# PSUM places for the second MLP matrix: a pair's three sums in three single banks, two-bank places kept for the inner tiles and the last transposes

## The chip, the cores and the metric

The kernel runs on one core of a Trainium2 chip. TensorE (PE in the profile) multiplies matrices and writes only to PSUM, the accumulation memory; VectorE (DVE) and ScalarE (ACT) read PSUM and do everything elementwise; GpSimd (POOL) does small elementwise work and issues some DMAs; SyncE (SP) issues the rest. Engines run on their own and wait for each other by semaphores. PSUM is used here in eight banks, each holding 512 floats for every one of 128 partitions. The metric is the time of one execution in device microseconds (us); less is better.

## The reference

One step of a decoder layer for 512 prompt tokens and 8 sample tokens (520 columns), width 1024, in float32. The change lies in the last part, the MLP and the final normalisation:

```python
h2 = _rmsnorm(x, norm2_g[l]) * (1.0 + sc2) + sh2
ff = jnp.square(jax.nn.relu(h2 @ w_ff1[l])) @ w_ff2[l]     # w_ff1 1024 x 4096, w_ff2 4096 x 1024
x = x + g2 * ff
y = _rmsnorm(x, final_norm_g)
```

The parts before it (a combined input projection, two recurrences, their merge and the output projection) are untouched.

## The kernel before

**Products.** Activations are kept transposed: features on partitions, the 520 tokens as columns, in two halves of 260 (`HALF`). Every float32 product is made of three faster ones, with the weight and the activation each split in a high and a low part: high by high, high by low, low by high (`products` L110, and the loop in `product` L1087). A weight tile comes by DMA into `wst`; ScalarE copies its high part (`whi`, L75), VectorE subtracts for the low part (`wlo`, L78). Smaller ones are `xhi` and `xlo` (L1033, L1036).

**The MLP in quarters.** The 4096 inner features are cut in four quarters `q` of eight tiles `j`. `unit(q, j, c)` (L1063) is a quarter of one inner tile: 12 matmuls into a two-bank place, one bank per half of the tokens; four of them make the tile. `hidden` (L1116) and `squared` (L1162) then evacuate it: a small ScalarE copy (`fsh`, L1159), a VectorE multiplication by the norm's factor (`ft`, L1172), ReLU and square on ScalarE. `formed` turns two tiles into seven combinations of them, for the next step.

**The second matrix, by seven products.** For each quarter, the output's eight 128-row tiles are taken in four pairs `m`. A pair by two halves of the tokens is a 2 by 2 block product, computed by Strassen's scheme (Winograd's form) with seven products instead of eight. Each product (`product`, L1074) is 12 matmuls of 128x128 by 128x260: four inner steps of three. The seven, numbered 1 to 7 in the code, go into three sums:

- sum 0: products 1, 6, 5, 3, one after the other onto the same accumulator,
- sum 1: products 7, then 4,
- sum A: product 2 alone.

Between two products of one sum, the intermediate value is read out: ScalarE copies it to SBUF (`snap`, L1098; L1106 scales, L1108 does the eight sample columns), after products 1, 6, 7 and 5. After 2 and 4 VectorE adds it to `x` at once (L1214), after 3 also (L1226, L1227). GpSimd adds the snaps to `x` by DMAs that accumulate (L1202, L1220).

**The order** is written out in `plan` (L916) and kept by `behind`, so TensorE runs the items in that order. In quarters 0 to 2, after the inner tiles, the products of pair `m` are woven with the last two of pair `m - 1`:

```python
prods(q, (0, 6), (0, 2), (0, 7), (0, 5))
for m in range(1, 4):
    prods(q, (m, 1), (m - 1, 4), (m - 1, 3), (m, 6), (m, 2), (m, 7), (m, 5))
units(q + 1, 1, 0)
prods(q, (3, 4), (3, 3))
```

Three units of the next quarter stand within this stretch, two after product (0, 1) and one before (3, 4). In the last quarter the order is another, since its last inner tile is needed soon after it is done: (0, 1) and (1, 1), then the first three inner steps of (0, 2), (1, 2), (0, 7), (1, 7), then their last steps, then the rest. `schedule` (L969) gives the item at which each weight is split; the order on ScalarE, VectorE and for other transposes follows from the compiler's own list schedule by priority, in which `urgent` (L149) moves instructions ahead.

**PSUM in the MLP.** The tile framework gives out places of pools and adds the waits. `ppt` and `ppb` have one bank each, `pmm` two places of two banks, and `pps`, two single banks, is closed at the start of the MLP so that `pm3`, a third two-bank place, can lie there (L1246). `place` (L1057) hands out the three two-bank places in turn: to the inner tiles, and to a pair for sums 0 and 1, one in each bank (`t[:, 0], t[:, 1]`, L1081). Sum A goes to `ppt` or `ppb` in turn.

**The end.** When a pair of output tiles is complete, `final_pair(m, s)` (L1302) transposes its 256 rows back to tokens for half `s` of the tokens, four transposes into bank `s` of one place per pair (`fplace`); ScalarE sums squares (L1318), VectorE multiplies by the final gain (`fx`, L1326). With `s` = 1 the samples follow in a bank of `ppt` (L1322 to L1325). `final_rows` (L1329) scales the rows and sends them out.

Of the kernel before, what the change touches and what calls it, by code (L numbers as in the profile page):

```python
# [6 lines left out]
F32 = mybir.dt.float32  # L7
# [4 lines left out]
OP = mybir.AluOpType  # L12
PSUM = bass.MemoryType.PSUM
# [3 lines left out]
L = 512  # L17
NB = 8
T = L + NB
HALF = T // 2  # L20
# [28 lines left out]
class Kernel:  # L49
# [19 lines left out]
    def _split_w(self, st, place, after=None):  # L69
        if place is None:  # L70
            hi, lo = (self.wst.tile([128, KO, 128], F32R, tag="wst", name=n) for n in ("whi", "wlo"))
        else:
            pool = self.sw if place % 2 else self.whl
            hi, lo = (pool.tile([128, KO, 128], F32R, tag=f"{n}{place}", name=n, bufs=1) for n in ("whi", "wlo"))
        ins = self.nc.scalar.copy(hi, st)  # L75
        if after:
            self.behind(ins, after)
        self.nc.vector.tensor_tensor(lo, st, hi.bitcast(F32), OP.subtract)  # L78
        return hi, lo
# [974 lines left out]
    def entry(self, key):  # L1054
        return self.ready[key[1:]]

    def place(self, n=None):  # L1057

        if n is None:
            n = self.nplace = (self.nplace + 1) % 3  # L1060
        return (self.pmm if n else self.pm3).tile([128, 2, 512], F32, name="mm")

    def unit(self, q, j, c):  # L1063

        if c == 0:
            self.upsum = self.place()
        hi, lo = self.entry(self.tile_key(q, j))
        for k in (2 * c, 2 * c + 1):
            last = self.last_product
            self.products(self.upsum, (hi[:, k], lo[:, k]), self.h2[k], k == 0, k == KO - 1, NM + 1, after=last)  # L1070
        if c == 3:
            self.hidden(q, j, self.upsum)

    def product(self, q, m, j, ks):  # L1074

        st = self.pairs.setdefault((q, m), {"s": {}})
        g, part = self.GROUP[j]
        hi, lo = self.entry(self.pair_key(q, m, g))
        if ks[0] == 0:
            if j == 1:  # L1080
                t = self.place((self.nplace + 2) % 3 if (q, m) == (3, 3) else None)  # L1081
                st["mm"] = t[:, 0], t[:, 1]
            if j == 2:
                st["A"] = (self.ppt.tile([128, 512], F32, name="pt") if m % 2 and (q, m) != (3, 3) else
                           self.ppb.tile([128, 512], F32, name="pb"))
        ps = (st["A"] if j == 2 else st["mm"][int(j in (7, 4))])[:, :HALF]
        for k in ks:  # L1087
            w, (ah, al) = 4 * part + k if g else k, self.ff[k]
            f = self.FORM[j]
            for n, (x, y) in enumerate(((hi, ah), (hi, al), (lo, ah))):  # L1090
                ins = self.nc.tensor.matmul(ps, x[:, w], y[:, f], start=j in (1, 7, 2) and k == 0 and n == 0,  # L1091
                                            stop=k == 3 and n == 2, skip_group_check=True)
                self.behind(ins, self.last_product)
                self.last_product = ins
        if ks[-1] == 3:
            self.added(q, m, j, ps, st["s"])
# [65 lines left out]
    def squared(self, q, j, ps, sh, halves):  # L1162
        nc = self.nc
        a, n = halves[0], len(halves)
        c = slice(a * HALF, (a + n) * HALF)
        if a == 0:
            self.ft = self.misc.tile([128, T], F32, name="ft", bufs=2)
        t, u = self.two(self.ft)[:, a:a + n], ps[:, a:a + n, :HALF]
        if q == 0 and j < 2:
            nc.scalar.copy(t, u)  # L1170
            u = t
        nc.vector.tensor_tensor(t, u, self.two(self.rs)[:, a:a + n], OP.mult)  # L1172
        t = self.ft[:, c]
        p = min(c.stop, L) - c.start
        nc.scalar.activation(t[:, :p], t[:, :p], AF.Relu, bias=sh[:, 0:1])  # L1175
        if c.stop == T:
            eng = nc.vector if j == KO - 1 else nc.gpsimd
            eng.tensor_tensor(t[:, p:], t[:, p:], sh[:, 1:9], OP.add)  # L1178
            eng.tensor_scalar(t[:, p:], t[:, p:], 0.0, None, OP.max)
        f = self.f8[:, 2 * (j % 2) + a:2 * (j % 2) + a + n]  # L1180
        nc.scalar.activation(f, self.two(self.ft)[:, a:a + n], AF.Square)  # L1181
# [54 lines left out]
    def mlp(self):  # L1236
        nc, tc = self.nc, self.tc
        self.close_pool()
        self.early.close()
        self.ffp = self.ctx.enter_context(tc.tile_pool(name="ffp", bufs=1, reuse_waits="tile"))  # L1240
        self.zs = self.consts.tile([128, KO, NB], F32, name="zs")
        nc.vector.memset(self.zs, 0.0)
        self.ng = self.consts.tile([128, KO], F32, name="ng")
        nc.vector.tensor_scalar(self.ng, self.modT[:, 40:48, 0], -1.0, None, OP.mult)
        self.ff, self.pairs = {}, {}
        self.pp.close()  # L1246
        self.pm3 = self.ctx.enter_context(tc.tile_pool(name="pm3", bufs=1, space=PSUM, reuse_waits="tile"))
        self.nplace, self.through, self.last_copy = 0, set(), None
        self.begin_weights()
        for n, (what, q, a, b, *ks) in enumerate(self.items):  # L1250
            self.ahead(n)
            if what == "u":
                self.unit(q, a, b)
                continue
            if what == "f":
                if q < 4:
                    self.ff[0] = self.ff_tiles(0)
                    self.formed(0, 0)
                    self.formed(0, 1)
                continue  # L1260
            if (q, a, b, ks[0][0]) == (3, 0, 1, 0):
                self.final_open()
            self.product(q, a, b, *ks)
# [38 lines left out]
    def final_pair(self, m, s):  # L1302


        nc = self.nc
        self.njunk = (self.njunk + 1) % 4
        junk = self.junk[:, self.njunk]
        if s == 0:
            self.fplace = self.place((self.nplace + (0 if m == 3 else 1)) % 3)
        p = self.fplace[:, s]  # L1310
        p4 = p.rearrange("p (t m f) -> p t m f", t=2, m=2)
        fs = slice(2 * m * 128, 2 * m * 128 + 256)
        for j in range(2):
            for t in range(2):
                c = (2 * s + t) * 128
                nc.tensor.transpose(p4[:, t, j], self.x[2 * m + j][:, c:c + 128], self.ident)
        for t in range(2):
            nc.scalar.activation(junk, p[:, 256 * t:256 * t + 256], AF.Square,  # L1318
                                 accum_out=self.fss[:, 2 * s + t, m:m + 1])
        if s:  # L1320
            p2 = self.ppt.tile([128, 512], F32, name="pt")
            for j in range(2):  # L1322
                nc.tensor.transpose(p2[:NB, j * 128:(j + 1) * 128], self.x[2 * m + j][:, L:], self.ident)
            nc.scalar.activation(junk[:NB], p2[:NB, :256], AF.Square, accum_out=self.fss[:NB, NC, m:m + 1])
            nc.vector.tensor_tensor(self.fxs[:, fs], p2[:NB, :256], self.gbc[:NB, fs], OP.mult)  # L1325
        nc.vector.tensor_tensor(self.fx[:, 2 * s:2 * s + 2, fs], p.rearrange("p (t f) -> p t f", f=256),  # L1326
                                self.gbc[:, None, fs].to_broadcast([128, 2, 256]), OP.mult)
# [19 lines left out]
    def run(self):  # L1347
        tc, i, enter = self.tc, self.i, self.ctx.enter_context
# [5 lines left out]
        self.ppt = enter(tc.tile_pool(name="ppt", bufs=1, space=PSUM))  # L1354
        self.ppb = enter(tc.tile_pool(name="ppb", bufs=1, space=PSUM))
        self.pmm = enter(tc.tile_pool(name="pmm", bufs=2, space=PSUM))
        self.pp = ExitStack()
        self.pps = self.pp.enter_context(tc.tile_pool(name="pps", bufs=2, space=PSUM))
        self.whl = enter(tc.tile_pool(name="whl", bufs=2))
        self.act = enter(tc.tile_pool(name="act", bufs=2))  # L1360
        self.early = ExitStack()
# [187 lines left out]
```

## Time and profile before

| | us |
|---|---|
| median of 3 runs | 1072.58 (1072.53 to 1072.72) |
| the profiled execution, its own time | 1072.83 |
| its span in the profile | 1070.8 |
| granted TensorE clock, mean | 0.996 |
| busy: PE, DVE, ACT, POOL | 1012.6, 696.0, 526.0, 112.0 |
| inner tiles of quarters 1 and 2, stretches of the span | 778.78 to 821.46, 874.73 to 917.43 |
| products of quarters 0, 1 and 2 | 725.49 to 778.78, 821.46 to 874.73, 917.43 to 970.72 |
| products of the last quarter | 1010.46 to 1058.75 |
| after the last product | 1058.75 to 1070.8 |

How to read it: the span counts from the first instruction of the program, and the execution's own time has about 2 us around it. "Busy" of PE is the union of its matmuls' durations, which overlap: a matmul of 260 columns is shown with 0.28 us, and in a steady stream one starts every 0.12 us. So a short idle time of PE in the rows stands for a somewhat longer loss of its rhythm. In the lists of waits, a row gives the waiting instruction, who released it, the sum of the idle time, the times it occurred and the longest.

### The profile page before, as it was taken

The numbers are of one execution on the slowest core, as the hardware profiler recorded it, in microseconds if no ns is written. First come the engines' busy times: TensorE is split into PE (matmuls) and PEld (weight loads), VectorE is DVE, ScalarE is ACT, GpSimd is POOL, SyncE is SP. The second block draws the span as 40 slices with busy tenths as digits, with TensorE's granted clock in tenths as the row PEclk, the third lists the DMA queues.
The fourth block names the chain that finished last, engine by engine and source line by source line (L and its number), as shares of the span: only waits on it lengthen the run. The fifth ranks groups of instructions, "written<-read, shape, count | busy, mean of one in ns | idle before, by whom it ended". The sixth has DMA issues, their size and how long they took to land.

```text
span 1070.8 us, 24259 instructions
## 1 busy us (share of the span) xinstructions
PE 1012.6 (95%) x9940; PEld 970.0 (91%) x9940; DVE 696.0 (65%) x1583; ACT 526.0 (49%) x1020; POOL 112.0 (10%) x215
## 2 busy tenths in 40 slices
PE   3899999999999999999999999999899889989995
PEld 1799999999999999999999999998899889989985
DVE  6568679596786867473333357766567656757765
ACT  5445744663574464351222244565456446545644
POOL 2200000000000000110000000022311321232030
PEclk9999999999999999999999999999999999999998
DMA  9963344344334335785555594224642562462142
GB/s 276 250 172 105 117 133 121 118 127 125 107 120 129 92 105 149 211 264 154 158 160 160 162 283 121 80 79 89 138 129 60 123 162 71 95 142 61 60 79 80
DMA packets 247792, 143.71 MB, mean 134 GB/s; under 512 B 6622, under 2 KB 242326, under 8 KB 247674
## 3 DMA queue, kind: packets, MB, share of 16 engines
q1 hardware_dynamic: 237874, 130.28, 42.7%
q0 software_dynamic: 9808, 11.89, 6.0%
q8 instruction: 78, 1.28, 0.5%
q14 instruction: 32, 0.26, 0.1%
HBM read 123.61 MB, written 11.26 MB: 126 GB/s over the span
## 4 chain that ended last, share of the span: by engine, by line
PE 87%; issue 3%; DMA 3%; ACT 3%; SPq 3%; DVE 2%; DVEq 0%; POOL 0%; ACTq 0%; POOLq 0%
PE mm L115 64%; PE mm L1091 11%; PE ps L356 2%; SPq L1441 2%; PE pb L702 1%; PE ps L561 1%; PE pb L1091 1%; ACT whi L75 1%; PE pt L1091 1%; DMA wst<-in_w_in_dram 1%; DMA wm<-in_w_mod_dram 1%; PE pt L645 1%; PE pt L634 1%; DVE ma L1214 1%; DMA wst<-in_w_out_dram 1%
## 5 line engine op out<-in xcount | busy, mean ns | idle before, releaser
L115 PE MATMUL mm<-h,whi 128*128 128x260 f32 (+1 forms) x3072 | 514.0, 286 | 1.4 <-ACT X L137 1.4
L115 PEld LDWEIGHTS mm<-h,whi 128*128 128x128 f32 x3072 | 427.3, 188 | 7.0 <-issue 3.4
L115 PE MATMUL mm<-h,wlo 128*128 128x260 f32 (+1 forms) x1536 | 316.4, 285 | 0.0
L75 ACT CAST whi<-wst 128x1024 fp32r<-128x1024 f32 x168 | 175.5, 1048 | 239.9 <-PE mm L115 173.9
L78 DVE TENSOR_TENSOR wlo<-wst,whi 128x1024 fp32r<-128x1024 f32 x168 | 205.1, 1221 | 115.8 <-ACT whi L75 114.6
L115 PEld LDWEIGHTS mm<-h,wlo 128*128 128x128 f32 x1536 | 239.9, 189 | 1.6 <-issue 1.0
L115 PE MATMUL mm<-a,whi 128*128 128x260 f32 x512 | 84.7, 285 | 0.0
L115 PEld LDWEIGHTS mm<-a,whi 128*128 128x128 f32 x512 | 70.6, 188 | 1.4 <-issue 1.4
L115 PE MATMUL mm<-a,wlo 128*128 128x260 f32 x256 | 52.3, 284 | 0.0
L1091 PE MATMUL mm<-ff0h,whi 128*128 128x260 f32 x80 | 26.0, 324 | 21.5 <-DVE ma L1214 13.6
L797 POOL DMA_DIRECT2D t<-oaT_d x8 | 4.3, 548 | 399.2 <-ACT ma L137 388.6
L1186 DVE TENSOR_TENSOR f<-f 128x260 f32<-128x260 f32 x64 | 27.3, 426 | 27.7 <-ACT f L1181 27.1
L115 PE MATMUL mm<-b,whi 128*128 128x260 f32 x256 | 41.8, 285 | 0.0
L1178 POOL TENSOR_TENSOR ft<-ft,fsh 128x8 f32<-128x8 f32 x28 | 17.5, 624 | 225.9 <-DVE ft L1172 225.9
L1175 ACT ACTIVATE ft<-ft,fsh 128x512 f32<-128x512 f32 (+2 forms) x36 | 23.9, 675 | 34.6 <-DVE ft L1172 34.6
L1091 PEld LDWEIGHTS mm<-ff0h,whi 128*128 128x128 f32 x80 | 15.0, 187 | 27.4 <-DVE ma L1214 16.5
L115 PEld LDWEIGHTS mm<-a,wlo 128*128 128x128 f32 x256 | 39.5, 188 | 0.2 <-issue 0.2
L115 PEld LDWEIGHTS mm<-b,whi 128*128 128x128 f32 x256 | 35.0, 188 | 1.6 <-issue 1.6
L1106 ACT ACTIVATE snap<-mm,ng 128x260 f32<-128x260 f32 (+1 forms) x30 | 14.3, 476 | 37.8 <-PE mm L1091 37.8
L1220 POOL DMA_DIRECT2D ma<-snap x28 | 25.6, 913 | 56.8 <-issue 41.0
L813 DVE TENSOR_TENSOR t<-mm,t 128x520 f32<-128x520 f32 x8 | 5.6, 699 | 36.7 <-PE ps L372 36.7
L1202 POOL DMA_DIRECT2D ma<-snap x28 | 25.0, 893 | 41.4 <-ACT snap L1108 17.9
(431 smaller groups left out, 1877.6 us busy)
## 6 DMA issues: line engine op xcount, KB each, us to landing
wst<-in_w_in_dram SPq DMA_DIRECT2D x64, 512.0 KB
wst<-in_w_mod_dram SPq DMA_DIRECT2D x32, 512.0 KB
wst<-in_w_ff_dram SPq DMA_DIRECT2D x64, 256.0 KB
wst<-in_w_ff_dram SPq DMA_DIRECT2D x32, 512.0 KB
wm<-in_w_mod_dram SPq DMA_DIRECT2D x16, 512.0 KB
st<-in_state_hgrn_dram SPq DMA_DIRECT2D x8, 512.0 KB
vb<-vd SPq DMA_DIRECT2D x8, 512.0 KB
out_dram<-st SPq DMA_DIRECT2D x8, 512.0 KB
```

Source lines behind the costliest of these rows:

```text
L75: ins = self.nc.scalar.copy(hi, st)
L78: self.nc.vector.tensor_tensor(lo, st, hi.bitcast(F32), OP.subtract)
L115: self.last_product = self.nc.tensor.matmul(ps[:, s, :c.stop - c.start], x, y[:, c], start=first and n == 0, stop=last and n == 2)
L356: nc.tensor.matmul(ps[r:r + 32, :n], self.cT[:, k, :], w[:, k, :], start=k < 4, stop=k >= KO - 4)
L1091: ins = self.nc.tensor.matmul(ps, x[:, w], y[:, f], start=j in (1, 7, 2) and k == 0 and n == 0, stop=k == 3 and n == 2, skip_group_check=True)
L1106: ins = self.nc.scalar.activation(t[:, :n], ps[:, :n], AF.Copy, scale=scale)
L1175: nc.scalar.activation(t[:, :p], t[:, :p], AF.Relu, bias=sh[:, 0:1])
L1178: eng.tensor_tensor(t[:, p:], t[:, p:], sh[:, 1:9], OP.add)
L1186: self.nc.vector.tensor_tensor(f[:, n], f[:, a], f[:, b], op)
L1202: nc.gpsimd.dma_start(x[1][:, b], v[:, :n], accum_op=OP.add)
L1220: nc.gpsimd.dma_start(x[t][:, a], s[p], accum_op=OP.add)
L1441: nc.sync.dma_start(raw[k][:, :, j * 128:(j + 1) * 128], w[r:r + 1024, c:c + 128].rearrange("(k p) n -> p k n", p=128))
```

## The change

PSUM in the MLP is laid out anew. `pps` stays open, and `pm3` and `place` go. Inner tiles take the two places of `pmm` in turn. A pair's three sums lie in three tiles of one bank each: sum 0 in `pps` (two banks, so two pairs may be open), sum 1 in `ppt`, sum A in `ppb`. Three sums of the last quarter, whose order keeps more of them open, take a whole `pmm` place and use its first bank. In the final step each `final_pair` takes a `pmm` place of its own, with the samples' transposes in its second bank, issued before the sums of squares instead of after. The multiplication that evacuates an inner tile is marked urgent for all tiles (before, for the last tile of a quarter alone).

```diff
     def unit(self, q, j, c):
         if c == 0:
-            self.upsum = self.place()
+            self.upsum = self.pmm.tile([128, 2, 512], F32, name="mm")
...
     def product(self, q, m, j, ks):
-        if ks[0] == 0:
-            if j == 1:
-                t = self.place((self.nplace + 2) % 3 if (q, m) == (3, 3) else None)
-                st["mm"] = t[:, 0], t[:, 1]
-            if j == 2:
-                st["A"] = (self.ppt.tile([128, 512], F32, name="pt") if m % 2 and (q, m) != (3, 3) else
-                           self.ppb.tile([128, 512], F32, name="pb"))
-        ps = (st["A"] if j == 2 else st["mm"][int(j in (7, 4))])[:, :HALF]
+        bank = {7: 4, 6: 1, 5: 1, 3: 1}.get(j, j)
+        if ks[0] == 0 and j in (1, 7, 2):
+            if (q, m, j) in ((3, 1, 7), (3, 1, 2), (3, 2, 1)):
+                st[bank] = self.pmm.tile([128, 2, 512], F32, name="mm")[:, 0]
+            else:
+                pool, name = {1: (self.pps, "ps"), 4: (self.ppt, "pt"), 2: (self.ppb, "pb")}[bank]
+                st[bank] = pool.tile([128, 512], F32, name=name)
+        ps = st[bank][:, :HALF]
...
     def squared(self, q, j, ps, sh, halves):
-        nc.vector.tensor_tensor(t, u, self.two(self.rs)[:, a:a + n], OP.mult)
+        with self.urgent():
+            nc.vector.tensor_tensor(t, u, self.two(self.rs)[:, a:a + n], OP.mult)
...
     def mlp(self):
-        self.pp.close()
-        self.pm3 = self.ctx.enter_context(tc.tile_pool(name="pm3", bufs=1, space=PSUM, reuse_waits="tile"))
...
     def final_pair(self, m, s):
-        if s == 0:
-            self.fplace = self.place((self.nplace + (0 if m == 3 else 1)) % 3)
-        p = self.fplace[:, s]
+        t = self.pmm.tile([128, 2, 512], F32, name="mm")
+        p, p2 = t[:, 0], t[:, 1]
...
+        if s:
+            for j in range(2):
+                nc.tensor.transpose(p2[:NB, j * 128:(j + 1) * 128], self.x[2 * m + j][:, L:], self.ident)
         for t in range(2):
             nc.scalar.activation(junk, p[:, 256 * t:256 * t + 256], AF.Square,
                                  accum_out=self.fss[:, 2 * s + t, m:m + 1])
         if s:
-            p2 = self.ppt.tile([128, 512], F32, name="pt")
-            for j in range(2):
-                nc.tensor.transpose(p2[:NB, j * 128:(j + 1) * 128], self.x[2 * m + j][:, L:], self.ident)
             nc.scalar.activation(junk[:NB], p2[:NB, :256], AF.Square, accum_out=self.fss[:NB, NC, m:m + 1])
```

More of the change, by code (lines that the diff above doesn't have):

```diff
@@ L1055, in entry @@
         return self.ready[key[1:]]
[L1057 to L1061, printed above, removed]
     def unit(self, q, j, c):
         if c == 0:
-            self.upsum = self.place()
+            self.upsum = self.pmm.tile([128, 2, 512], F32, name="mm")
         hi, lo = self.entry(self.tile_key(q, j))
@@ L1245, in mlp @@
         self.ff, self.pairs = {}, {}
-        self.pp.close()
-        self.pm3 = self.ctx.enter_context(tc.tile_pool(name="pm3", bufs=1, space=PSUM, reuse_waits="tile"))
-        self.nplace, self.through, self.last_copy = 0, set(), None
+        self.through, self.last_copy = set(), None
         self.begin_weights()
@@ L1356, in run @@
         self.pmm = enter(tc.tile_pool(name="pmm", bufs=2, space=PSUM))
-        self.pp = ExitStack()
-        self.pps = self.pp.enter_context(tc.tile_pool(name="pps", bufs=2, space=PSUM))
+        self.pps = enter(tc.tile_pool(name="pps", bufs=2, space=PSUM))
         self.whl = enter(tc.tile_pool(name="whl", bufs=2))
```

## The prediction

> **What bounds the kernel now.** I read the page first: who is busy, what the chain that ended last consists of, and the costliest groups.
>
> ```profile
> span 1070.8 us, 24259 instructions
> ...
> PE 1012.6 (95%) x9940; PEld 970.0 (91%) x9940; DVE 696.0 (65%) x1583; ACT 526.0 (49%) x1020; POOL 112.0 (10%) x215
> ...
> PE 87%; issue 3%; DMA 3%; ACT 3%; SPq 3%; DVE 2%; DVEq 0%; POOL 0%; ACTq 0%; POOLq 0%
> ...
> L1091 PE MATMUL mm<-ff0h,whi 128*128 128x260 f32 x80 | 26.0, 324 | 21.5 <-DVE ma L1214 13.6
> ```
>
> TensorE is the bound: 87% of the chain. Only one group of matmuls has much idle time before it: the first matmul of a product of the second matrix (L1091, inner step 0, high by high), 21.5 us. The reader is to see that such a product starts late because VectorE or ScalarE still reads a sum. Next the waits of PE, first for quarters 0 to 2, then for the last quarter:
>
> ```profile
> PE mm L1091 <- DVE ma L1214: 12.0, 12, 1.5
> PE mm L1091 <- ACT snap L1108: 7.5, 12, 0.6
> ```
>
> ```profile
> PE mm L1316 <- DVE fx L1326: 1.8, 1, 1.8
> PE mm L1091 <- DVE ma L1214: 1.6, 2, 0.9
> PE mm L1091 <- ACT snap L1108: 0.3, 1, 0.3
> PE mm L1091 <- DVE wlo L78: 0.3, 1, 0.3
> ```
>
> 12 and 12 over three quarters of four pairs: two waits in every pair. Then the timeline shows which. PE's rows around one wait of each kind (pair 0 of quarter 2), then ScalarE's:
>
> ```profile
> 925.99 0.28 PE L1091 MATMUL mm<-ff3h,wlo 128*128 128x260 f32 x1
> 926.91 0.39 PE L1091 MATMUL mm<-ff0h,whi 128*128 128x260 f32 x1 [0.63 <-ACT snap L1108]
> 927.13 0.28 PE L1091 MATMUL mm<-ff0l,whi 128*128 128x260 f32 x1
> 927.25 0.28 PE L1091 MATMUL mm<-ff0h,wlo 128*128 128x260 f32 x1
> ...
> 932.43 0.39 PE L1091 MATMUL mm<-ff0h,whi 128*128 128x260 f32 x1 [0.96 <-DVE ma L1214]
> ```
>
> ```profile
> 926.32 0.47 ACT L1106 ACTIVATE snap<-mm,modT 128x252 f32<-128x252 f32 x1
> 926.68 0.17 ACT L1108 ACTIVATE snap<-mm 128x8 f32<-128x8 f32 x1
> 928.64 0.47 ACT L1106 ACTIVATE snap<-mm,ng 128x252 f32<-128x252 f32 x1 [1.79 <-PE mm L1091]
> 929.07 1.05 ACT L75 CAST whi<-wst 128x1024 fp32r<-128x1024 f32 x1
> 930.08 0.48 ACT L1106 ACTIVATE snap<-mm,modT 128x260 f32<-128x260 f32 x1
> ```
>
> The matmul of 926.91 opens product (0, 5), in bank 0 of the pair's place. The reading that it waits for (926.32, 926.68; scaled by `modT`, with the samples apart, so after product 7) is of bank 1 of that place. What (0, 5) truly needs, the snap after product 6, is long done. At 932.43 product (0, 3), again in bank 0, waits for the addition after (0, 4), in bank 1. A product on a fresh tile does not wait: by twelve matmuls a product, (1, 1) ran from 928.4 on, while the 928.64 snap read the other place. So the waits come from two sums that share one tile.
>
> **What a wait costs.** Rhythm counts, not idle time: 0.12 us from start to start (927.13, 927.25). From 925.99 to 927.13 stand two starts, 1.14 us for 0.24, so 0.90 us is lost where the row says 0.63: 0.27 more. The sum is made by stretches:
>
> ```profile
> 725.49:778.78 53.29, 46.79 (x375) 45.11 (x374) 32.70 (x54) 27.02 (x53) 16.82 (x26) 1.00 0.55 121
> 778.78:821.46 42.68, 42.68 (x351) 42.68 (x350) 29.89 (x47) 23.62 (x38) 6.17 (x12) 1.00 0.36 97
> 821.46:874.73 53.27, 46.74 (x374) 45.07 (x373) 32.68 (x54) 27.02 (x53) 17.15 (x26) 1.00 0.54 120
> ...
> 917.43:970.72 53.29, 46.75 (x374) 45.08 (x373) 32.70 (x54) 27.02 (x53) 16.75 (x26) 1.00 0.58 125
> ...
> 1010.46:1058.75 48.29, 45.98 (x372) 44.15 (x370) 32.91 (x68) 26.09 (x70) 10.44 (x20) 1.00 0.26 56
> ```
>
> The columns are length, then busy time of PE, weight loads, DVE, ACT and POOL, PE's clock, DMA share and GB/s. The inner stretch of the second row is free of waits: 29 units of 12 matmuls in 42.68 us, 0.1226 each. An unhindered product in the chain:
>
> ```profile
> 853.19 1.45 PE mm L1091 x12
> ```
>
> **The change part by part.**
>
> *Sums 0 and 1 in tiles of their own.* A product stretch holds 28 products and three units: 28 x 1.45 + 36 x 0.1226 = 45.0 us. The stretches last 53.29, 53.27 and 53.29, so 8.3 us are lost in each, **24.9 us** in three. From the waits: 19.5 us idle and 24 x 0.27 = 6.5, 26.0. I take 25.4, between the two. In the last quarter three such waits go: 1.6 + 0.3 + 3 x 0.27 = **2.7 us**.
>
> Here a page may be weighed. The Trainium skill (Perfetto Trace Analysis, Identifying the Most-Contended Engine) says that busy time of matmuls misjudges headroom, since they are pipelined, and that the busy share of weight loads is to be used. By matmuls the three stretches would give 3 x 6.5 = 19.5 us, by weight loads 3 x 8.2 = 24.6; the rhythm worked out above sides with the weight loads.
>
> *What is late next where the waits go.* (0, 5) needs the snap after 6, with two products between, 2.9 us; (0, 3) needs the snap after 5, also with two between, and 928.64 + 0.47 + 0.17 is over by 929.3. Sum 1 in one bank: (m, 7) needs the addition after (m - 1, 4), with three between, 4.3 us; before, that wait was for the product after it. Sum A in `ppb` alone: seven products. `pps` has two banks, so (m, 1) needs (m - 2, 3), six products. The engines have room: in 45 us VectorE's 32.7 us is 73%, ScalarE's 27.0 is 60%, GpSimd's 17 with the DMAs of the snaps 38%; SyncE's weight loads follow the splits as before, and the DMA share of 0.55 to 0.58 becomes 0.65 to 0.69.
>
> *The second weight part.* It sets a new distance. VectorE's rows in the same pair:
>
> ```profile
> 930.15 1.23 DVE L78 TENSOR_TENSOR wlo<-wst,whi 128x1024 fp32r<-128x1024 f32 x1 [3.37 <-ACT whi L75]
> 931.30 0.68 DVE L1036 TENSOR_TENSOR xlo<-wst,xhi 128x512 fp32r<-128x512 f32 x1
> 931.90 0.48 DVE L1214 SCALAR_TENSOR_TENSOR ma<-mm,modT,ma 128x260 f32<-128x260 f32 x1
> ```
>
> The weight split at 929.07 takes the place that (0, 5) has freed, is ready at 931.38 and is first needed by (1, 6), one product after 932.43: 933.98 and two matmuls more, 934.22. That leaves 2.8 us. Without the wait of 932.43 (0.96 + 0.27) it is 1.6 us: still there, so 0 lost. If VectorE's order puts two of its other steps ahead (1.23 + 0.68 = 1.9), 0.3 us is late per weight.
>
> *In the last quarter* one late weight exists:
>
> ```profile
> 1043.08 0.38 ACT L1104 COPY snap<-mm 128x260 f32<-128x260 f32 x1 [1.00 <-PE mm L1091]
> 1043.35 1.05 ACT L75 CAST whi<-wst 128x1024 fp32r<-128x1024 f32 x1
> ...
> 1044.43 1.23 DVE L78 TENSOR_TENSOR wlo<-wst,whi 128x1024 fp32r<-128x1024 f32 x1
> ...
> 1045.71 0.39 PE L1091 MATMUL mm<-ff0h,wlo 128*128 128x260 f32 x1 [0.25 <-DVE wlo L78]
> ```
>
> The product between, (2, 4), waited for the snap of 1043.08 by the same sharing. That goes, and this wait grows by as much, for the weight follows that snap: 0.
>
> *Inner tiles in two places instead of three.* A tile must be read out before the tile after next starts, one tile later, 48 x 0.1226 = 5.9 us:
>
> ```profile
> 902.45 0.41 PE L115 MATMUL mm<-h,wlo 128*128 128x260 f32 x2
> ...
> 904.88 0.69 DVE L1172 TENSOR_TENSOR ft<-mm,rs 128x520 f32<-128x520 f32 x1
> ```
>
> The first row holds a tile's last matmuls, which end at 902.86; its reading ends at 905.57: 2.7 us of 5.9. Cost 0, and the urgent mark moves the reading ahead of a `wlo`, by up to 1.2 us; the weight parts that then come later have whole tiles of time. If that cover went, it would cost the rival below.
>
> *The last transposes.* Their places become single-use, and the end after 1058.75 holds one wait that goes:
>
> ```profile
> 1042.84 0.60 PE L1316 MATMUL mm<-ident,ma 128*128 128x128 f32 x4
> ...
> 1046.05 0.68 DVE L1326 TENSOR_TENSOR fx<-mm,fin 128x512 f32<-128x512 f32 x1
> ...
> 1059.25 0.46 DVE L1226 SCALAR_TENSOR_TENSOR ma<-mm,modT,ma 128x252 f32<-128x252 f32 x1
> ...
> 1060.70 0.16 DVE L1232 TENSOR_TENSOR ma<-ma,zs 128x8 f32<-128x8 f32 x1
> 1060.77 0.65 PE L1316 MATMUL mm<-ident,ma 128*128 128x128 f32 x4 [1.80 <-DVE fx L1326]
> ```
>
> The last four transposes could start at 1059.75, after L1226: 1.0 us. But the samples' two, now in the same tile and ahead of the sums of squares, need L1232, which ends at 1060.86. If sharing a tile holds readers back as it holds writers back, the squares start when they do now. So the bound below is -1.0. Above: pair 2's sum holds one `pmm` place until (2, 3), six products of 1.45 or 8.7 us after the first transposes, and three sets of transposes share the other, 3.9 us each from 1042.84 to 1046.73, 11.7 in all: +3. I take 0, near the row of L1232.
>
> Sum, against the profiled execution's own 1072.83 us (span 1070.8 and 2 us around it; 0.25 above the median of 1072.58): 1072.83 - 25.4 - 2.7 = **1044.7 us**.
>
> **The rivals.**
>
> *Late weights take the place of the waits.* For: the distance falls to 1.6 us, and VectorE is 73% busy. Against: ScalarE and VectorE follow PE's progress in these rows, and 1.6 us holds one whole subtraction. With two further steps ahead, 0.3 us at each of two weights in 12 pairs is 7 us; with three (3.1 us), 1.5 x 24 = 36 would be more than is gained, so I price the middle, 0.3 to 0.6: 1052 to 1059 us.
>
> *The inner tiles wait for their places: slower.* The Trainium skill (Perfetto Trace Analysis, Optimization Strategy) holds that equal gaps that repeat can mean too few PSUM buffers; by that rule the waits of before would come from too few places, and a change that takes the third away from the inner tiles would bring more. As a mechanism here: each of 29 tiles loses what its reading takes beyond 5.9 us after its end. It decides from 5.9 on, and for slower than before it must reach about 6.9 us (29 x 1.0 = 29 us). The row has 2.7, so VectorE would need three to four more subtractions of 1.23 ahead of each reading; at 7.0 us the time is 1044.7 + 32 = 1077. Against: the gaps stand between products of a place already held, and no unit waits.
>
> *It doesn't do what it says:* the waits follow the two readers and not the shared tile, and stay: 1072. For: the rows alone show times, no tiles. Against: the fresh tile that didn't wait.
>
> **How the numbers follow.** The forecast 0.80 (own range 1043 to 1048: 24.9 or 26.0 for the stretches, -1.0 and +3 at the end); late weights 0.14; the rest unchanged 0.03, slower 0.03. The range reaches from 1042.5 to 1052, the near end of the late weights. 0.2% is 2.1 us, about what a measurement of this kernel can tell from no change: faster 0.94, within 0.03, slower 0.03.
>
> **What would show it.** Right: no row of PE waiting for L1214 or L1108 in the product stretches, these 45 us long, the inner stretch still 42.7, VectorE and ScalarE with the same busy time. Wrong: PE's idle rows at L1091 with `wlo` L78 (late weights); at L115 with `ft` L1172 (places); the end after the last product longer than 12.05 us (transposes).

## The result and the profile after

The changed kernel takes **1044.69 us** (median of 4 runs, 1043.90 to 1044.86) against 1072.65 us before (4 runs, 1072.53 to 1075.74): a ratio of 0.9731, 95% interval 0.9713 to 0.9749. The profiled execution's own time is 1044.54 us. Two executions differ by a few us before the MLP (673.6 to 677.2 us in the kernels below) and hardly at all in it, so single us are read from stretches of the span and not from medians.

The page of the changed kernel, busy times and the chain:

```profile
span 1042.6 us, 24269 instructions
...
PE 1005.1 (96%) x9940; PEld 968.5 (93%) x9940; DVE 694.9 (67%) x1583; ACT 526.1 (50%) x1020; POOL 112.8 (11%) x215
...
PE 90%; DMA 3%; SPq 3%; ACT 1%; DVE 1%; issue 1%; DVEq 0%; ACTq 0%
```

VectorE, ScalarE and GpSimd have the work that they had (694.9 for 696.0, 526.1 for 526.0, 112.8 for 112.0). Their shares of the chain shrink: ScalarE from 3% to 1%, VectorE from 2% to 1%. Busy PE fell by only 7.5 us while the span fell by 28.2, so PE's busy time doesn't tell the gain.

PE's waits from 640 us to the end, all that are left:

```profile
PE ps L1085 <- DVE wlo L78: 1.1, 1, 1.1
PE mm L1308 <- DVE zs L1222: 0.7, 1, 0.7
PE mm L1311 <- DVE ma L1227: 0.6, 1, 0.6
PE pt L1085 <- DVE ff3l L1108: 0.3, 1, 0.3
```

L1085 is the matmul that was L1091, L1209 and L1102 are the two readers that were L1214 and L1108: neither releases PE anywhere. Before, there were 14 and 13 such waits. The new layout's stretches (length, then busy time of PE, weight loads, VectorE, ScalarE, GpSimd, PE's clock, DMA share, GB/s):

```profile
725.14:769.79 44.65, 44.65 (x374) 44.65 (x373) 30.53 (x52) 26.96 (x53) 15.03 (x25) 1.00 0.63 137
769.79:812.49 42.70, 42.70 (x350) 42.70 (x349) 31.60 (x49) 23.61 (x38) 7.93 (x14) 1.00 0.39 105
812.49:857.14 44.65, 44.65 (x374) 44.65 (x373) 30.53 (x52) 26.95 (x53) 15.22 (x25) 1.00 0.63 137
...
899.84:944.50 44.66, 44.66 (x375) 44.66 (x373) 30.54 (x52) 26.96 (x53) 15.32 (x25) 1.00 0.62 137
984.24:1030.08 45.84, 44.42 (x370) 43.86 (x369) 33.23 (x70) 26.43 (x71) 11.79 (x20) 1.00 0.28 59
1030.08:1042.56 12.48, 1.45 (x10) 0.70 (x8) 6.32 (x17) 4.11 (x13) 0.00 (x0) 0.68 0.44 171
```

In the product stretches (first, third and fourth row) PE's busy time equals the length: not one gap. Where the 28.3 us between the two profiled executions went (the span before ends at 1070.84):

| stretch | before | after | difference | predicted |
|---|---|---|---|---|
| products of quarters 0, 1, 2 | 53.29, 53.27, 53.29 | 44.65, 44.65, 44.66 | -25.9 | -25.4 |
| products of the last quarter | 48.29 | 45.84 | -2.45 | -2.7 |
| after the last product | 12.09 | 12.48 | +0.4 | 0 |
| inner stretches between | 42.68 | 42.70 | 0 | 0 |

The rest, 0.35, lies before the MLP. How pair 0 of quarter 2 now runs, all engines in order of time:

```profile
908.53 0.28 PE L1085 MATMUL ps<-ff0h,whi 128*128 128x260 f32 x1
908.73 0.47 ACT L1100 ACTIVATE snap<-pt,modT 128x252 f32<-128x252 f32 x1
...
911.68 1.23 DVE L78 TENSOR_TENSOR wlo<-wst,whi 128x1024 fp32r<-128x1024 f32 x1 [2.48 <-ACT whi L75]
...
912.86 0.28 PE L1085 MATMUL ps<-ff0h,whi 128*128 128x260 f32 x1
...
913.43 0.48 DVE L1209 SCALAR_TENSOR_TENSOR ma<-pt,modT,ma 128x260 f32<-128x260 f32 x1
...
914.54 0.28 PE L1085 MATMUL ps<-ff0h,wlo 128*128 128x260 f32 x1
```

These are the two products whose waits the prediction quoted. (0, 5) opens at 908.53, ahead of the reading after product 7 (908.73, from `pt`) that it used to wait for; (0, 3) opens at 912.86, ahead of the addition after (0, 4) (913.43). The second weight part is ready at 911.68 + 1.23 = 912.91 and asked for at 914.54: 1.63 us to spare, where 1.6 were predicted.

The late weight of the last quarter, around the wait of 1.1 us:

```profile
1013.66 0.41 DVE L1317 TENSOR_TENSOR fin<-mm,fin 8x256 f32<-8x256 f32 x1
1014.00 0.67 DVE L1318 TENSOR_TENSOR fx<-mm,fin 128x512 f32<-128x512 f32 x1
1014.60 0.67 DVE L1048 TENSOR_TENSOR wst<-wst 128x512 f32<-128x512 f32 x1
...
1015.05 0.38 ACT L1098 COPY snap<-mm 128x260 f32<-128x260 f32 x1 [1.00 <-PE mm L1085]
...
1015.33 1.05 ACT L75 CAST whi<-wst 128x1024 fp32r<-128x1024 f32 x1
...
1016.45 0.49 DVE L1209 SCALAR_TENSOR_TENSOR ma<-pt,modT,ma 128x260 f32<-128x260 f32 x1
...
1016.81 0.28 PE L1085 MATMUL ps<-ff0l,whi 128*128 128x260 f32 x1
...
1016.93 1.22 DVE L78 TENSOR_TENSOR wlo<-wst,whi 128x1024 fp32r<-128x1024 f32 x1
...
1018.20 0.39 PE L1085 MATMUL ps<-ff0h,wlo 128*128 128x260 f32 x1 [1.11 <-DVE wlo L78]
1018.43 0.28 PE L1085 MATMUL ps<-ff1h,whi 128*128 128x260 f32 x1
```

This weight is made by sums of weights (L1045 to L1048), and VectorE put two multiplications of the final step (L1317, L1318) ahead of the last of them, which ends at 1015.27. On ScalarE the copy (1015.33) stands behind the snap of 1015.05, so the sum and the snap both hold it to about 1015.3. It ends at 1016.38, but the subtraction starts only at 1016.93: VectorE does the addition L1209 (1016.45) and one small step first. Before, the subtraction (1044.43) started as the copy ended (1044.40), and that addition came behind it, at 1045.65. From 1016.81 to 1018.43 stand two starts, 1.62 us for 0.24: 1.38 us lost.

After the last product, the last transposes and the first squares:

```profile
1031.22 0.63 PE L1308 MATMUL mm<-ident,ma 128*128 128x128 f32 x4 [0.71 <-DVE zs L1222]
...
1032.24 0.16 DVE L1227 TENSOR_TENSOR ma<-ma,zs 128x8 f32<-128x8 f32 x1
...
1032.45 0.38 PE L1311 MATMUL mm<-ident,ma 128*8 128x128 f32 x2 [0.59 <-DVE ma L1227]
...
1032.87 0.38 ACT L1313 ACTIVATE fin<-mm 128x256 f32<-128x256 f32 x1 [0.22 <-PE mm L1311]
...
1034.72 0.67 DVE L1318 TENSOR_TENSOR fx<-mm,fin 128x512 f32<-128x512 f32 x1
```

The four transposes came as early as foreseen, 1.14 us after the last product's end at 1030.08. But the sums of squares wait for the samples' two, which lie in the other bank of the same tile: they start 2.79 us after the last product; before, at 1061.46, 2.71 us after it.

### The profile page after: what moved, and what is told of

The parts are those of the page before. It is cut to its first block, busy times and chain, and to the rows that moved or that the text cites. A ratio compares the mean times of both kernels' runs of the same rounds, so it can differ in the third digit from the quotient of the medians.

```text
span 1042.6 us, 24269 instructions
## 1 busy us (share of the span) xinstructions
PE 1005.1 (96%) x9940; PEld 968.5 (93%) x9940; DVE 694.9 (67%) x1583; ACT 526.1 (50%) x1020; POOL 112.8 (11%) x215
## 4 chain that ended last, share of the span: by engine, by line
PE 90%; DMA 3%; SPq 3%; ACT 1%; DVE 1%; issue 1%; DVEq 0%; ACTq 0%
PE mm L115 65%; PE ps L1085 8%; PE pt L1085 4%; PE pb L1085 2%; PE ps L356 2%; SPq L1432 2%; PE pb L702 1%; PE ps L561 1%; DMA wst<-in_w_branch_a_dram 1%; DMA wst<-in_w_in_dram 1%; DMA wm<-in_w_mod_dram 1%; PE mm L1085 1%; PE pt L645 1%; PE pt L634 1%; PE ps L529 1%
## 5 line engine op out<-in xcount | busy, mean ns | idle before, releaser
L115 PE MATMUL mm<-h,whi 128*128 128x260 f32 (+1 forms) x3072 | 513.9, 286 | 1.4 <-ACT X L137 1.4
L115 PEld LDWEIGHTS mm<-h,whi 128*128 128x128 f32 x3072 | 427.3, 188 | 7.0 <-issue 3.4
L115 PE MATMUL mm<-h,wlo 128*128 128x260 f32 (+1 forms) x1536 | 316.4, 285 | 0.0
L115 PEld LDWEIGHTS mm<-h,wlo 128*128 128x128 f32 x1536 | 240.0, 189 | 1.5 <-issue 1.0
L115 PE MATMUL mm<-a,whi 128*128 128x260 f32 x512 | 84.6, 285 | 0.0
L115 PEld LDWEIGHTS mm<-a,whi 128*128 128x128 f32 x512 | 70.6, 188 | 1.4 <-issue 1.4
L115 PE MATMUL mm<-a,wlo 128*128 128x260 f32 x256 | 52.3, 284 | 0.0
L1181 DVE TENSOR_TENSOR f<-f 128x260 f32<-128x260 f32 x64 | 27.3, 427 | 28.3 <-ACT f L1176 27.6
L115 PE MATMUL mm<-b,whi 128*128 128x260 f32 x256 | 41.8, 285 | 0.0
L115 PEld LDWEIGHTS mm<-a,wlo 128*128 128x128 f32 x256 | 39.5, 188 | 0.2 <-issue 0.2
L115 PEld LDWEIGHTS mm<-b,whi 128*128 128x128 f32 x256 | 35.0, 188 | 1.6 <-issue 1.6
L1215 POOL DMA_DIRECT2D ma<-snap x28 | 27.2, 971 | 35.2 <-issue 30.9
L1197 POOL DMA_DIRECT2D ma<-snap x28 | 26.2, 935 | 43.6 <-DMA ma<-snap 28.1
L1176 ACT ACTIVATE f<-ft 128x520 f32<-128x520 f32 (+1 forms) x36 | 20.8, 587 | 14.4 <-POOL ft L1174 12.3
L376 DVE TENSOR_REDUCE mods<-ps 128x9 f32<-128x36 f32 x32 | 6.1, 192 | 31.4 <-PE ps L372 31.3
L115 PE MATMUL mm<-b,wlo 128*128 128x260 f32 x128 | 25.9, 283 | 0.0
```

Of the source, the lines that this page charges most:

```text
L115: self.last_product = self.nc.tensor.matmul(ps[:, s, :c.stop - c.start], x, y[:, c], start=first and n == 0, stop=last and n == 2)
L1181: self.nc.vector.tensor_tensor(f[:, n], f[:, a], f[:, b], op)
L1197: nc.gpsimd.dma_start(x[1][:, b], v[:, :n], accum_op=OP.add)
L1215: nc.gpsimd.dma_start(x[t][:, a], s[p], accum_op=OP.add)
```

## The experiments

**One pairing put back.** The theory: two sums in one tile are what makes the waits, whichever two they are. Sums 1 and A get the two banks of one tile; sum 0, until now in `pps`, goes to `ppt` and `ppb` in turn; the two banks of `pps` become the one tile, `pab`. So the old pairing stays apart, and one that neither kernel had is made.

```diff
-                pool, name = {1: (self.pps, "ps"), 4: (self.ppt, "pt"), 2: (self.ppb, "pb")}[bank]
-                st[bank] = pool.tile([128, 512], F32, name=name)
+                if bank == 1:
+                    pool, name = (self.ppb, "pb") if m % 2 else (self.ppt, "pt")
+                    st[1] = pool.tile([128, 512], F32, name=name)
...
+                elif "pair" not in st:
+                    st["pair"] = self.pab.tile([128, 2, 512], F32, name="pa")
+                    st[4], st[2] = st["pair"][:, 0], st["pair"][:, 1]
```

> The changed kernel, but sums 1 and A of a pair lie in the two banks of one tile (in the two banks of pps), and sum 0 in ppt or ppb in turn; no two sums share a bank. Theory (a reader of any bank of a tile holds back the next product into that tile's other bank): each pair gets one new wait, product (m, 7) for the addition L1214 of before that follows (m, 2), some 0.9 to 1.2 us of PE's rhythm each, in 14 to 15 places: 1057 to 1062 us, and no wait for the snaps. Rival 'the number of places': inner tiles and sums have as many places as in the changed kernel, so 1044.7 us. Rival 'the readers themselves are what PE waits for': they read as before, nothing changes, 1044.7 us.

Measured: 1061.49 us (1060.85 to 1061.89, 4 runs), a ratio of 0.9893 to before (0.9877 to 0.9910). PE's longest row of waits in the MLP, and the window of the first product stretch:

```profile
PE pa L1091 <- DVE ma L1215: 12.7, 14, 1.6
```

```profile
726.15:775.50 49.35, 45.69 (x374) 44.95 (x373) 30.50 (x52) 26.96 (x53) 15.79 (x25) 1.00 0.56 124
```

A new wait for the addition stands in every pair of the first three quarters and twice in the last, 14 in all, now before a matmul into `pa`, the shared tile. The stretch is 4.70 us longer than in the changed kernel (44.65): four pairs at 0.91 + 0.27 = 1.18 us each, 4.7. That settles the theory: the waits go where the sharing goes. Each sum, and the inner tiles, have as many banks here as in the changed kernel, and the readers are the same, so both rivals fall.

**The urgent mark alone, both ways.** Once the change without the mark at L1167 (the lines below), once the kernel before with it:

```diff
-        with self.urgent():
-            nc.vector.tensor_tensor(t, u, self.two(self.rs)[:, a:a + n], OP.mult)
+        nc.vector.tensor_tensor(t, u, self.two(self.rs)[:, a:a + n], OP.mult)
```

> The changed kernel without the urgent mark at the reading of an inner tile (it stays at the last tile of a quarter, as before the change). Theory (sharing is all): the reading takes 2.7 us of the 5.9 that two places leave it, so 1044.7 us, within 0.5. Rival 'the reading's delay is what cost time, and the mark cured it': back towards 1072, at the least by 1 us for each quarter, 1049 and more.

> The kernel before, with the urgent mark of the change as its only edit. Theory (sharing is all): 1072.6 us, within 0.6, with the 27 waits for L1214 and L1108 still there. Rival 'the mark brings the gain or a part of it': 1050 to 1068.

Measured: 1044.62 us without the mark (1044.43 to 1047.11), the product stretches 44.65, 44.66 and 44.66 and PE's four waits as above (the last quarter's products took 46.21 us, 0.4 more, in the profiled execution, the slowest of the four); 1073.11 us for the kernel before with it, a ratio of 1.0005 (0.9994 to 1.0015). The mark is worth nothing that the medians show in either; the gain is the layout's.

**A place taken from the inner tiles.** One of the two places of `pmm` is held by an idle tile until the last inner tile is done, to measure the cover on which the second place was costed at 0.

```diff
+        hold = self.pmm.tile([128, 2, 512], F32, name="mm")
+        nc.vector.memset(hold[:, 0, 0:1], 0.0)
```

> The changed kernel, with one of the two pmm places held from the start of the MLP to the end of the last inner tile by a tile of no use, so that inner tiles have one place. Theory: each of some 28 tiles then waits for the whole reading of the one before, 1.5 to 2.7 us and 0.3 of rhythm each, 50 to 85 us in all: 1095 to 1130 us, with PE waiting at L115 for ft. It sizes the cover that two places give. Rival 'places were never short for the inner tiles, one would do': 1045 us. Rival 'the third place was what counted before': then already the changed kernel would show waits at L115, and one place costs about twice what it showed, nothing.

Measured: 1168.89 us in one run, 124 us more than the changed kernel, well above the range. Its waits for the reading of an inner tile, then a whole inner stretch and the product stretch after it:

```profile
PE mm L115 <- DVE ft L1167: 70.8, 26, 2.9
PE mm L115 <- ACT ft L1164: 3.9, 2, 2.9
```

```profile
805.96:880.74 74.78, 55.22 (x350) 53.76 (x349) 35.13 (x59) 26.96 (x47) 5.09 (x14) 0.84 0.25 67
880.74:925.56 44.82, 44.82 (x374) 44.82 (x373) 27.24 (x41) 24.04 (x44) 14.88 (x24) 1.00 0.58 125
```

The wait is the one expected: 28 of them, 74.7 us, up to 2.9 each (the prediction read 2.7 of 5.9 us as used). So the mechanism of the slower rival exists, and with two places it has 5.9 us of cover against it. But 74.7 is not 124. The seventh column shows the rest: the clock was 0.84 in the inner stretch, 1.00 in the products. Windows cut after one wait, that ends at 813.40, show it directly:

```profile
813.40:814.90 1.50, 1.50 (x12) 1.50 (x13) 0.04 (x1) 1.38 (x3) 0.42 (x2) 0.96 0.70 202
814.90:818.20 3.30, 3.30 (x16) 3.30 (x16) 2.14 (x5) 1.65 (x2) 0.00 (x0) 0.50 0.33 100
818.20:819.30 1.10, 1.10 (x10) 1.10 (x10) 0.87 (x1) 0.00 (x0) 0.00 (x0) 1.00 0.00 0
```

The middle window is at 0.50 throughout, and the 0.96 of the first stands for 0.1 us more: about 3.4 us at half the clock. In the 3.3 us, 16 matmuls start where 27 would (3.3 / 0.1226): 1.35 us lost; by the clock it is 1.7 (half of 3.4). The trace shows 26 such drops, one for each gap of 2.75 to 2.93 us, each 3.4 us long and beginning 0 to 1.5 us after the gap's end; the two gaps of 1.0 us have none. Seven drops in the inner stretch of 74.78 us give its mean of 0.84. So the 124 us are 74.7 of idle time, 28 x 0.27 = 7.6 of rhythm and 26 x 1.35 to 1.7 = 35 to 44 of clock, 117 to 126 in all. The expectation had the first two terms and left the clock out.

**The samples' transposes in a tile of their own.** They go to a bank of `pps` and again stand after the sums of squares, so the squares should not wait for them.

```diff
-        p, p2 = t[:, 0], t[:, 1]
+        p = t[:, 0]
...
-        if s:
-            for j in range(2):
-                nc.tensor.transpose(p2[:NB, j * 128:(j + 1) * 128], self.x[2 * m + j][:, L:], self.ident)
...
+            p2 = self.pps.tile([128, 512], F32, name="ps")
+            for j in range(2):
+                nc.tensor.transpose(p2[:NB, j * 128:(j + 1) * 128], self.x[2 * m + j][:, L:], self.ident)
```

> The changed kernel, with the samples' transposes of final_pair in a bank of pps of their own and issued after the sums of squares, as before the change. Theory (a tile is held back as a whole, for readers too): the last sums of squares no longer wait for the samples' update of x, so the stretch after the last product, 12.5 us, falls by 0.9 to 1.6 us: 1043.1 to 1043.8 us. Rival 'the squares wait for the rows themselves': no change, 1044.7 us.

Measured: 1043.97 us (1043.68 to 1045.14), ratio 0.9736 (0.9723 to 0.9749). The stretch after the last product is 12.74 us, not shorter. Its timeline (here the last product ends at 1028.93), and then the same last two rows of the changed kernel:

```profile
1030.38 0.38 ACT L1310 ACTIVATE fin<-mm 128x256 f32<-128x256 f32 x1
...
1033.35 2.96 SPq L1334 DMA_DIRECT2D out_dram<-fx  x4
...
1036.41 1.08 SPq L1337 DMA_DIRECT2D out_dram<-fin  x1
```

```profile
1033.67 3.97 SPq L1334 DMA_DIRECT2D out_dram<-fx  x4
...
1037.72 0.69 SPq L1337 DMA_DIRECT2D out_dram<-fin  x1
```

The step did what it should: the last squares start 1.45 us after the last product instead of 2.79, so they had waited for the samples' transposes in the same tile and not for the rows. The forecast time was missed all the same, for the gain is gone by the outputs. The last issue begins 7.48 us after the last product instead of 7.64, and lasts 1.08 us instead of 0.69, so SyncE is through at 8.56 us instead of 8.33. The issue before it, the fourth of `fx`, took 1.00 us instead of 0.38. Here the third `fx` issue follows the second by 0.88 us instead of 2.49, and its own 0.33 us is unchanged. Why the two after it are longer then is not settled.

**Two marks that moved nothing.** To settle the late weight, the sums of weights of the last pair were marked urgent; for the 0.3 us wait for `ff3l`, the last two combinations of the last quarter; a third kernel held both and the samples' edit.

```diff
+            with self.urgent() if (q, m) == (3, 3) else ExitStack():
...
+            with self.urgent() if q == 3 else ExitStack():
```

> The changed kernel, with the four sums of weights (L1045 to L1048) of the last pair of the last quarter marked urgent. Theory: the late weight before product (3, 6), 1.1 us of PE's idle time, comes from these sums standing behind other work on VectorE; the weight's split then starts at once after its sum, and the wait falls to 0.3 us or less: 1043.5 to 1043.9 us. Rival 'the split waits for a snap or a place on ScalarE': unchanged, 1044.7 us.

> The changed kernel, with the last two of the seven combinations of the last inner tile's halves marked urgent in the last quarter, ahead of two weight splits. Theory: PE's wait for ff3l before the last inner step of (0, 7), 0.57 us of rhythm, goes: 1044.1 us, within 0.3. Rival: the two weights that then come later make (0, 6) or (1, 6) wait instead (they have 3.5 us to spare), 1044.7 us or more.

> The changed kernel with the three edits together: samples apart, weight sums first, forms first. Theory: the gains add up, 0.9 to 1.6 and 0.8 to 1.2 and 0.5: 1041.4 to 1042.5 us, a ratio to before of 0.971 to 0.972. Rival: what is gained before the last product is given back after it, for the end hangs on VectorE, which is then more crowded: 1043.5 us or more.

Measured: 1044.89 (1044.14 to 1045.64), 1044.31 (1043.54 to 1044.97) and 1044.47 us (1043.51 to 1044.92). The first and the third missed. The second lies in its range by luck, for the wait that was to go is there. The two waits stayed at 1.1 and 0.3 us, because VectorE's order in the rows stayed as it was: the two multiplications still stood ahead of the last sum, two weight splits ahead of the last combinations. In the third kernel the samples' edit worked as it does alone, and the waits were 0.9 and 0.3 us. These runs say nothing on the cause; they only show that a mark is not an order. What would be gained at `ff3l` remains open.

**The sum of weights put ahead by an order.** Now the two multiplications are made to follow L1048.

```diff
-            nc.vector.tensor_tensor(x12, x12, x22, OP.add)
+            self.behind(self.gain, nc.vector.tensor_tensor(x12, x12, x22, OP.add)) if (q, m) == (3, 3) else nc.vector.tensor_tensor(x12, x12, x22, OP.add)
...
-            nc.vector.tensor_tensor(self.fxs[:, fs], p2[:NB, :256], self.gbc[:NB, fs], OP.mult)
+            self.gain = nc.vector.tensor_tensor(self.fxs[:, fs], p2[:NB, :256], self.gbc[:NB, fs], OP.mult)
```

> The changed kernel, with the last sum of the weights of pair (3, 3) put ahead of the two multiplications by the final gain that stood before it on VectorE (an order, no mark). Theory: the late weight of the last quarter is late because VectorE makes the sum that it is split after only at 1014.60, behind these two; ahead of them its copy on ScalarE can start about 1014.4 instead of 1015.33 and the subtraction end about 1016.7 instead of 1018.15, before TensorE asks for it at about 1017.1. So PE's wait for wlo (1.1 us) goes or falls under 0.3, and the stretch of the last quarter's products falls from 45.84 to 44.5 to 44.9; the time to 1043.3 to 1043.8. Rival: the weight is late because its place is freed late or its transfer lands late; then the wait stays at 1.1 and the stretch at 45.8.

Measured: 1043.43 us (1042.64 to 1046.69, 4 runs), ratio 0.9734 (0.9718 to 0.9749). The timeline of the same weight, then the windows of the last quarter's products and of the end:

```profile
1013.72 0.69 DVE L1048 TENSOR_TENSOR wst<-wst 128x512 f32<-128x512 f32 x1
...
1014.45 1.05 ACT L75 CAST whi<-wst 128x1024 fp32r<-128x1024 f32 x1 [0.43 <-DVE wst L1048]
...
1015.40 0.37 ACT L1098 COPY snap<-mm 128x260 f32<-128x260 f32 x1
...
1015.52 1.23 DVE L78 TENSOR_TENSOR wlo<-wst,whi 128x1024 fp32r<-128x1024 f32 x1 [0.19 <-ACT whi L75]
...
1016.89 0.30 PE L1085 MATMUL ps<-ff0h,wlo 128*128 128x260 f32 x1
```

```profile
984.20:1028.65 44.45, 44.14 (x370) 43.79 (x369) 32.77 (x69) 26.39 (x71) 11.77 (x20) 1.00 0.29 60
1028.65:1041.33 12.68, 1.44 (x10) 0.71 (x8) 6.68 (x17) 4.10 (x13) 0.00 (x0) 0.71 0.43 168
```

The weight is ready at 1016.75, PE takes it at 1016.89 without a wait, and the stretch is 1.39 us shorter, the 1.38 that the wait had cost. The rival (place or transfer late) falls. More than the sum has moved, though: the copy now waits for the sum alone and stands ahead of the snap (1015.40) that it followed, and the subtraction stands ahead of the addition L1209. So the run shows that the wait goes when the weight is made earlier, and not how much of it was the sum's alone. The end is 0.2 us longer, so the whole kernel's median is 1.3 us under the changed kernel's, which these runs can't tell apart from it (the two intervals overlap almost wholly).

**The last output on another engine.** On top of the samples' edit, GpSimd issues the samples' output, so that SyncE's last issue is not behind four others; a second kernel has the ordered sum as well.

```diff
-            nc.sync.dma_start(self.o["y_s"][:, 0], self.fxs)
+            nc.gpsimd.dma_start(self.o["y_s"][:, 0], self.fxs)
```

> The kernel with the samples' transposes apart, and the output of the samples issued by GpSimd instead of SyncE. Theory: that kernel's rows were scaled 0.8 us earlier after the last product, and the gain was lost in SyncE's last two issues, which took 1.00 and 1.08 us instead of 0.38 and 0.69; on two engines the last issue ends about 1.1 us earlier, and the stretch after the last product falls from 12.74 to 11.6 to 12.0; the time to about 1043.3. Rival: the issue is slow because the transfers before it fill what both engines share, or GpSimd's own issue takes as long: the stretch stays at 12.5 to 13.

> Both edits in one kernel (the samples' transposes apart with their output on GpSimd, the sum of the weights ahead). Each theory's gain in its own stretch: the last quarter's products at 44.3 to 44.9, the end at 11.6 to 12.0, the time at 1042 to 1042.8, which would be 0.2% below the changed kernel. If the two rivals hold: 45.6 and 12.5 to 13, the time as the changed kernel's.

Measured: 1047.66 us (1046.75 to 1048.04, 5 runs), ratio 0.9765 (0.9752 to 0.9778), and 1047.05 us (1046.00 to 1047.60, 4 runs), ratio 0.9760 (0.9747 to 0.9774): slower than the changed kernel. The end lasts 15.84 and 16.20 us, longer than the theories and the rivals had it. SyncE's last waits in the first of the two, and GpSimd's row:

```profile
SPq L1529 <- DMA out_dram<-fin: 4.1, 1, 4.1
SPq L1529 <- PEq L1529: 3.6, 2, 3.1
```

```profile
1037.30 0.60 POOL L1337 DMA_DIRECT2D out_dram<-fin  x1 [28.78 <-DVE fin L1336]
```

The issue is earlier, as meant: it ends at 1037.90, 7.49 us after the last product (1030.41) instead of 8.56. But the program's end (L1529) waits 4.1 us for the transfer, where the samples' edit alone and the changed kernel have one of 2.7, and then 3.6 us for another engine, where they have 0.7. The row names PE, but PE waits there as SyncE does, and both go on when GpSimd is through: the trace has GpSimd's DRAIN, an instruction of the program's end, from 1037.27 to 1045.47, 8.20 us, and 8.20 us in the second kernel too. In the changed kernel GpSimd's longest is 4.42 us and begins at 1007.7, so it is over long before the end. -1.1 + 1.4 + 2.9 is +3.2; measured +3.1. In the second kernel the last quarter's products took 44.45 us again, which confirms the ordered sum once more. No version found here beats the changed kernel by more than the runs scatter.

## Why the prediction was right

**The waits come from two sums in one tile.** Right, and shown: the rows of pair 0 open ahead of the two readers, and the run with another pairing has a wait of the same kind at the new place. The rival that the change doesn't do what it says (1072) had the readers as the cause; the readers are unchanged.

**The size, 25.4 us for three product stretches.** Measured 25.9. Of the two figures it lay between, the one from the waits (26.0) was nearer, so 0.27 us of lost rhythm beside each idle time was a good term; the stretch of 45.0 us by products and units was 0.35 too long. The Trainium skill (Perfetto Trace Analysis, Identifying the Most-Contended Engine) held that headroom is read from the weight loads and not from the matmuls; 24.6 and 19.5 against 25.9 agree with it.

**The second weight part.** Right: 1.63 us left, no row of PE waiting for `wlo` in quarters 0 to 2. The late weights as a rival (1052 to 1059) needed two further steps of VectorE ahead, and in these quarters they didn't come: VectorE stood idle for 2.48 us before the split of 911.68, waiting for its copy. It is busy 30.5 of 44.65 us, 68% and not the 73% reckoned, since about 2 us of its work moved to the inner stretches (31.60 for 29.89).

**The last quarter, -2.7.** Measured -2.45, and the sum was closer than its terms, which is luck. By PE's starts the three waits that went were worth 2.63 us, as forecast, and two short ones went that the 2.7 doesn't hold, before (2, 4) and before the transposes of 1050.84, 0.33 and 0.30. The step that failed is "this wait grows by as much, for the weight follows that snap: 0". The wait for the late weight grew from 0.25 + 0.27 = 0.52 us of lost rhythm to 1.38, by 0.86 and not by the 0.33 of (2, 4). PE comes to it 0.35 us sooner, which was foreseen. The weight itself is ready 0.5 us later, which was not: the copy follows its snap as before, but VectorE now does an addition and a small step between the copy and the subtraction (0.55 us, before 0.03). This is the mechanism of the late weights' rival, other steps of VectorE ahead of the split, at a place where it wasn't looked for. The run with the sum ahead gives 1.39 us back; the split into 0.35 and 0.5 is read from rows, and no run separates it. The wait for `ff3l` grew by 0.3 us and is in no step of the prediction. Together this makes 2.1 of the 2.45; the rest lies in breaks of PE's rhythm too short to assign.

**The inner tiles in two places: 0.** Right. With one place PE waits for each reading, up to 2.9 us, as the 2.7 read from the rows had it; with two, no L115 waits. The price of losing the cover was read too low in that run's expectation: the clock falls as well. The Trainium skill (Perfetto Trace Analysis, Optimization Strategy) reads equal gaps that repeat as possibly too few buffers in PSUM. Here they repeated 24 times with three two-bank places and are gone with two, out of the same eight banks: in this case the trace does not bear it out, since the waiting products stood in a place that they already held, and what counted was which sums share a tile.

**The urgent mark.** Costed at nothing, and the medians of the two runs show nothing.

**The last transposes: 0.** Measured +0.4: 0.08 is the squares' start, and by the rows the 0.3 more is that VectorE now multiplies the samples first (L1317), so that the tile's own multiplication (L1318) comes 1.85 us after the squares' start instead of 1.22 (1061.46 to 1062.68 before); no run isolates this. The working held: the transposes came earlier, and a shared tile held the readers back as it had held the writers. That the lower bound of -1.0 could not be had by undoing the sharing alone was not foreseen: the squares were 1.34 us earlier in that run, and the outputs took it back.

## What to carry to other kernels

Where the accumulator of one unit waits for the reader of another, see from the names in the rows whether the two lie in one tile: the dependence may be on the tile and not on the data, and then smaller tiles out of the same banks take the wait away. Cost each such wait by the rhythm of starts and not by its idle time (here 0.27 us more). When waits go from the busiest engine, look at each later transfer or split that it now reaches sooner, back to the first instruction that it depends on, and at what the engine that makes it does first, for that is where some of the gain is given back.

## What the runs showed of the hardware

- In the run with one place for the inner tiles, each of 26 gaps of 2.75 to 2.93 us on TensorE brought its granted clock down to 0.50 for 3.4 us, beginning 0 to 1.5 us after the gap; two gaps of 1.0 us in the same run, and the waits of up to 1.5 us in the product stretches before the change, left it at 1.00. The Trainium skill (TensorE: Matmul & The Clock Gate, Why this matters for your kernels) asks for "No PE-idle gaps >~3µs between matmul bursts"; the rows agree in kind and show it just under that.
- An output of 32 KB issued by GpSimd at the program's end was waited for 4.1 us, one issued by SyncE 2.7, and the wait for the other engines at the end rose from 0.7 to 3.6 us, behind a DRAIN of 8.20 us on GpSimd.
- When SyncE's third output issue began 0.88 us after the second instead of 2.49, the two issues behind it took 1.00 and 1.08 us instead of 0.38 and 0.69.
